# First tokens without the shift, and Fourier blocks with four products side by side

## The chip, the cores and the metric

The kernel runs on one core of one Trainium2 chip. Its time is the device time of one execution in microseconds (us). Before the change it took 2610.99 us (median of 3 runs, 2606.53 to 2611.72). The engines are TensorE (PE; PEld is its weight load), VectorE (DVE), ScalarE (ACT), GpSimd (POOL) and SyncE (SP); DMA queues of SP, ACT and POOL feed them.

## The reference

The kernel computes one block of a diffusion backbone, batch 1, 2048 latent tokens of 1024 channels, 256 context tokens. The part around the change:

```python
sh1, sc1, g1, sh2, sc2, g2 = ada_mod(c, w_ada, b_ada)   # silu(c) @ w_ada + b_ada, six pieces of 1024
hx = rms_norm(x, norm1_g) * (1 + sc1) + sh1
fx, qx, kx, vx = split_projection(hx @ w_in)            # four pieces of 512 columns
y_four = fourier_mix(fx)                                # 4 groups x 128 channels, fft2, real part
y_attn = neighbourhood_attention(rope(norm(qx)), rope(norm(kx)), vx, kc, vc, rpb)
mixed = merge(hx, y_four, y_attn, w_branch_gate, ...)   # gates = sigmoid(hx @ w_branch_gate)
x = x + g1 * mixed
x = x + g2 * sqrelu_mlp(rms_norm(x, norm2_g) * (1 + sc2) + sh2, w_mlp1, w_mlp2)
```

The context tokens give kc and vc in the same way, modulated by c_ctx.

## The kernel before, in words

**Tiling.** Channels lie on the 128 partitions in 8 chunks k, tokens in four groups of 512 ("quads"). A product of float32 values is three matmuls of high and low halves (`mm3`, the matmul itself is at L85): high by high, high by low, low by high. Halves are float16 scaled by powers of two, except for the first 512 tokens, whose products are made of fp32r halves that need no scale.

**Start.** `vec` gathers c, c_ctx, the gains and b_ada by five small transfers (L659 to L663, SP's queue); it is transposed (L680) and `sil` = silu(c) is made (L686). `ada_load` brings a 1 MB tile of w_ada, 8 input chunks by 256 columns; `ada_sum` multiplies the first chunks by sil on DVE and adds them (L278, L280, and L281 for the two partial sums); `ada_cols` lets PE take the other chunks as single-column products (L291), sum DVE's part over the partitions (L292), and DVE adds bias and gain (L294, L295). The result is column k of `AB`: columns 0 to 7 the shift, 8 to 15 the scale. Before, each of the 8 tiles holds 128 shift and 128 scale columns of one chunk, and from the third tile on DVE takes 6 input chunks and PE 2 (`PE_K = 6`).

**First 512 tokens.** `load_x` fetches 128 tokens, squares them (L201 on DVE, L203 on ACT), POOL takes the power (L175), and the tokens are scaled (L206, L208). `hx_k` makes chunk k of the modulated tokens: four transposes (L217), high half and full value on ACT with scale and shift (L220, L222), low half on DVE (L225). Then 12 products of that chunk go into four PSUM banks, `ps_first0` to `ps_first3` (128 Fourier channels each), with the first Fourier weights `w_first` in fp32r halves (L90, L93). So the first tokens run chunk by chunk, 96 products, as fast as the modulation columns arrive.

**Other tokens.** `norm_scale` (L250 to L263) finds the power of two for AB once all columns are there. `load_unit` does the same for 256 columns of weights: squares (L473), a power on POOL (L474), a sum over partitions on PE (L479), halves on ACT (L492) and DVE (L493). `build` makes the float16 halves of a quad: four transposes per chunk (L233), scale and shift on DVE or ACT (L237, L239), high half on ACT (L240), low half on DVE (L241). `unit_T` multiplies: one bank of 128 output channels at a time, 24 matmuls over all 8 chunks, and `put_T` (L501) takes the bank to memory. `first_tokens` rescales the first quad into float16 halves (L765, L767, L768).

**Order.** `run_pair(0)` takes the Fourier weights over quads 1, 2, 3, four banks after one another per quad, while the next quad is loaded and built. `run_pair(1)` to `run_pair(7)` take the other weights two units at a time over quads 0, 1, the context, 2, 3: gates, then q, v, k with gates among them. `side_work` (modulation for the context and the second sub-layer, 32 loads of MLP weights for scales, tile `w12m`, L324 to L328) is fed in between by `tick`. A scheduler estimates when each instruction could run and so sets the order of instructions on every engine; `tc.issue_after` pins one instruction behind another. PSUM has 4 banks for products ("mm"), 2 for transposes ("tp") and 1 for modulation sums, scales and other small results ("ad").

Of the kernel before, what the change touches and what calls it, by code (L numbers as in the profile page):

```python
# [66 lines left out]
def dit_block(ctx: ExitStack, tc: tile.TileContext, a, out, taps=None, upto=9):  # L67
# [126 lines left out]
    def load_x(src, r0, name, xh=None, sq_on_dve=False, scale_on_dve=False):  # L194
        if xh is None:
            xh = pb.tile([128, D], F32, tag="xh", name=f"xh_{name}", bufs=5)
        load(xh, src[r0:r0 + 128, :])
# [7 lines left out]
        if scale_on_dve:  # L205
            dve.tensor_scalar(out=xh, in0=xh, scalar1=rs, scalar2=None, op0=ALU.mult)  # L206
        else:
            act.activation(xh, xh, AF.Copy, scale=rs)  # L208
        return xh

    def hx_k(xhs, k, hx, ab, name, t_on_act=False):

        hH, hL = hx
        w = hH.shape[2]
        tp = tpp.tile([128, 512], F32, tag="tp", name=f"tp_{name}_{k}")[:, :w]
        for i, xh in enumerate(xhs):
            pe.transpose(tp[:, i * 128:(i + 1) * 128], xh[:, k * 128:(k + 1) * 128], ident)  # L217
        sc, bi = ab[:, 8 + k:9 + k], ab[:, k:k + 1]
        t = pb.tile([128, 512], F32, tag="ht", name=f"ht_{name}_{k}", bufs=2)[:, :w]
        h_ = act.activation(hH[:, k, :], tp, AF.Identity, bias=bi, scale=sc)  # L220
# [63 lines left out]
    def ada_cols(dst, j, c0, gain, name, acc, wt=None, nk=KT):  # L284

        ps = adp.tile([128, 512], F32, tag="ad", name=f"ad{name}")
        for i in range(2):
            bs = slice(i * 128, (i + 1) * 128)

            for k in range(nk, KT):  # L290
                pe.matmul(ps[:, i:i + 1], wt[:, k, bs], sil[:, k:k + 1], start=(k == nk), stop=False)  # L291
            pe.matmul(ps[:, i:i + 1], acc[:, bs], ones[:, 0:1], start=(nk == KT), stop=True)  # L292
# [2 lines left out]
        dve.scalar_tensor_tensor(out=dst[:, 8 + j:9 + j], in0=dst[:, 8 + j:9 + j], scalar=1.0, in1=gain,  # L295
                                 op0=ALU.add, op1=ALU.mult)
# [1685 lines left out]
```

## Time and profile before

| | before |
|---|---|
| median of 3 runs | 2610.99 us |
| the profiled execution | 2607.65 us, its span 2605.9 us |
| mean granted TensorE clock | 0.992 |
| PE busy / DVE / ACT / POOL | 96% / 70% / 45% / 17% |
| instructions | 42107 |
| last of the first-token products begins | 59.74 us |
| first product of quad 1 begins | 62.67 us |
| first gate product (`run_pair(1)`) begins | 158.9 us |

All times below are microseconds from the span's start. In rows of the timeline the columns are start, duration, engine, line, operation, out<-in, partitions, shape, type, count, and in brackets the idle time before it with what ended it; a row with a count above 1 is a run of equal instructions. A float32 product stands in the trace as two matmul records, a transpose or a 512-wide product as one: for a table of which PE takes two input chunks the program has per half two products of L291 and one of L292, and the trace shows x4 and x2. The change touches only the first 160 us of the span directly; the other 2446 us come after it.

### The profile page before, as it was taken

How to read it: one execution, taken by the hardware profiler on the slowest of the kernel's cores; microseconds unless marked ns; L12 is line 12 of the kernel's file. 1: busy time of each engine (PE TensorE's matmuls, PEld its weight loads, DVE VectorE, ACT ScalarE, POOL GpSimd, SP SyncE). 2: the span in 40 equal slices, each digit the busy share in tenths (PEclk: the TensorE clock that was granted, in tenths of full speed). 3: DMA queues.
4: the chain of work that ended last, by engine and by line, in shares of the span. 5: the costliest groups of instructions: out<-in, count | busy, mean ns of one | idle time of the engine just before them, and what ended most of it. 6: DMA issues, size and time to landing. Idle time of an engine off the chain costs nothing.

```text
span 2605.9 us, 42107 instructions
## 1 busy us (share of the span) xinstructions
PE 2512.3 (96%) x15839; PEld 1445.3 (55%) x15839; DVE 1814.5 (70%) x3738; ACT 1169.0 (45%) x2086; POOL 449.9 (17%) x560
## 2 busy tenths in 40 slices
PE   7899989899999899999999999999999999999999
PEld 5445656777655577786665444444444444444444
DVE  7656996686454788996775787979777534546367
ACT  5533236453144588883444655546360423224150
POOL 1210211002212447630000121211212000000000
PEclk9899999999999999999999999999999999999999
DMA  6456688773174586745667877776876433333334
GB/s 276 125 208 204 198 282 304 251 248 126 49 255 164 137 245 177 198 133 196 227 221 264 272 259 250 246 259 226 294 256 210 144 99 105 94 109 97 106 104 155
DMA packets 223125, 506.39 MB, mean 194 GB/s; under 512 B 31732, under 2 KB 85756, under 8 KB 207816
## 3 DMA queue, kind: packets, MB, share of 16 engines
q1 hardware_dynamic: 189960, 384.57, 45.7%
q0 software_dynamic: 26176, 87.90, 9.7%
q10 hardware_dynamic: 6784, 31.21, 3.6%
q8 instruction: 124, 2.03, 0.3%
q14 instruction: 81, 0.66, 0.1%
HBM read 366.22 MB, written 137.38 MB: 193 GB/s over the span
## 4 chain that ended last, share of the span: by engine, by line
PE 71%; DMA 11%; DVE 10%; ACT 4%; issue 3%; POOL 1%; SPq 1%; ACTq 0%; DVEq 0%; POOLq 0%
PE p L85 21%; PE pm L85 19%; PE ps_g L85 8%; PE po L85 5%; DMA w12m<-in_w_mlp 3%; PE ps_k L85 3%; PE pua L85 2%; PE tp L1413 2%; PE ps_f L85 2%; PE pv L1427 2%; PE pmf L1348 1%; DMA vt<-v 1%; PE sc L1391 1%; DVE wo L375 1%; PE ps_q L85 1%
## 5 line engine op out<-in xcount | busy, mean ns | idle before, releaser
L85 PE MATMUL pm<-hc,wb 128*128 128x512 f16 x2688 | 582.6, 379 | 5.5 <-DVE u L1697 3.5
L85 PE MATMUL p<-wb,a 128*128 128x512 f16 x2688 | 581.9, 379 | 2.0 <-DVE X L1697 1.5
L85 PEld LDWEIGHTS <-wb 128*128 128x128 f16 x2688 | 263.0, 98 | 323.5 <-issue 7.2
L85 PEld LDWEIGHTS <-a 128*128 128x128 f16 x2688 | 263.0, 98 | 319.7 <-issue 2.9
L85 PE MATMUL ps_g<-hx,w_g 128*128 128x512 f16 x1536 | 345.5, 380 | 1.0 <-DVE qn_q L563 1.0
L1697 DVE TENSOR_TENSOR X<-X,p 128x512 f32<-128x512 f32 x280 | 183.8, 682 | 171.0 <-PE p L85 151.7
L85 PEld LDWEIGHTS <-hx 128*128 128x128 f16 x2304 | 226.6, 99 | 36.1 <-issue 3.6
L85 PEld LDWEIGHTS <-w_g 128*128 128x128 f16 x1536 | 150.8, 100 | 167.6 <-issue 4.4
L85 PE MATMUL po<-wo,mH 128*128 128x512 f16 x512 | 152.4, 379 | 0.3 <-DVE ga L1471 0.3
L1697 DVE TENSOR_TENSOR u<-pm,u 128x512 f32<-128x512 f32 x128 | 87.3, 688 | 84.5 <-PE pm L85 82.4
L374 ACT ACTIVATE wo<-ws,msc 128x512 f16<-128x512 f32 x96 | 69.0, 718 | 163.7 <-DVE ws L415 128.2
L1400 DVE CUSTOM_DVE_ANT_0 s<-sc,bt,qsc 128x736 f32<-128x736 f32 (+5 forms) x128 | 111.1, 868 | 22.4 <-PE sc L1394 16.8
L1701 ACT ACTIVATE p<-pm 128x512 f32<-128x512 f32 x32 | 18.9, 589 | 239.7 <-PE pm L85 239.7
L1421 DVE SCALAR_TENSOR_TENSOR pL<-tp,pH 128x640 f16<-128x640 f32 (+1 forms) x128 | 112.3, 878 | 11.8 <-ACT pH L1416 11.0
L501 ACT ACTIVATE ot_g<-ps_g,usc_g 128x512 f32<-128x512 f32 x64 | 43.7, 683 | 164.5 <-PE ps_g L85 158.9
L1831 POOL DMA_DIRECT2D xr<-x1d x32 | 17.2, 539 | 569.4 <-DVE X L1697 563.1
L1404 ACT ACTIVATE s<-s,m 128x736 f32<-128x736 f32 (+5 forms) x128 | 104.6, 817 | 15.6 <-DVE m L1400 15.4
L1413 PE MATMUL tp<-ident,s 128*128 128x128 f32 x704 | 102.5, 279 | 3.8 <-ACT s L1404 3.7
L374 ACT ACTIVATE wo<-raw,msc 128x512 f16<-128x512 f32 x128 | 87.6, 709 | 38.1 <-issue 23.5
L375 DVE SCALAR_TENSOR_TENSOR wo<-raw,msc,wo 128x512 f16<-128x512 f32 x128 | 94.1, 744 | 8.4 <-ACT wo L374 8.4
L85 PE MATMUL po<-wo,mL 128*128 128x512 f16 x256 | 97.0, 379 | 0.0
L1416 ACT ACTIVATE pH<-tp 128x640 f16<-128x640 f32 (+1 forms) x128 | 95.8, 748 | 0.5 <-PE tp L1413 0.5
(568 smaller groups left out, 4369.4 us busy)
## 6 DMA issues: line engine op xcount, KB each, us to landing
wb<-w1d SPq DMA_DIRECT2D x224, 256.0 KB
wb<-w2d SPq DMA_DIRECT2D x224, 256.0 KB
w12m<-in_w_mlp SPq DMA_DIRECT2D x32, 1024.0 KB
raw<-in_w_mlp ACTq DMA_DIRECT2D x24, 1024.0 KB
w1d<-wo POOLq DMA_DIRECT2D x84, 256.0 KB, 3.8
w2d<-wo POOLq DMA_DIRECT2D x84, 256.0 KB, 4.0
gT<-ot_g SPq DMA_DIRECT2D x64, 256.0 KB
hc<-hcd SPq DMA_DIRECT2D x14, 1024.0 KB
```

The costliest lines, as they stand in the source:

```text
L85: last_mm[0] = pe.matmul(ps, l, r, start=(start and i == 0), stop=(stop and i == n - 1))
L374: act.activation(hi, src, AF.Copy, scale=scale)
L375: dve.scalar_tensor_tensor(out=lo, in0=src, scalar=scale, in1=hi, op0=ALU.mult, op1=ALU.subtract)
L501: last_out[0] = act.activation(o, ps, func, scale=scale)
L1348: pe.matmul(ps, l, r, start=(i == 0), stop=(i == len(prods) - 1))
L1400: tail["dve"] = dve.tensor_tensor_reduce(out=s[:, :n], in0=sc, in1=bias, op0=ALU.add, op1=ALU.min, scale=qsc[:, 4:5], scalar=3.0e38, accum ...
L1404: tail["act"] = act.activation(s[:, :n], s[:, :n], AF.Exp, bias=m1[:, 0:1], scale=-1.0, accum_out=m1[:, 1:2])
L1413: tail["pe"] = pe.transpose(tp[:, i * 128:(i + 1) * 128], s[:, o:o + 128], ident)
L1416: tail["act"] = act.activation(pH[:, :c], tp[:, :c], AF.Copy, scale=PTOP)
L1421: tail["dve"] = dve.scalar_tensor_tensor(out=pL[:, :c], in0=tp[:, :c], scalar=PTOP, in1=pH[:, :c], op0=ALU.mult, op1=ALU.subtract)
L1427: tail["pe"] = pe.matmul(pv, p_[:nk, i * 128:(i + 1) * 128], vv[:nk, h2 * 128 + o:h2 * 128 + o + 64], start=(j == 0 and i == 0), stop=(j = ...
L1697: last["dve"] = dve.tensor_tensor(out=o, in0=x, in1=y, op=op)
```

## The change

**Modulation tables.** They are packed so that tiles 0 to 3 hold 256 scale columns each (two chunks) and tiles 4 to 7 hold 256 shift columns each. `ada_cols` fills two scale columns or two shift columns per call. The share of input chunks that DVE sums becomes `PE_K = (0, 4, 6, 6, 4, 2, 0, 0)`, PE takes the rest: 0 means that PE does all 8.

**First tokens.** `hx_k` multiplies by the scale alone. The shift's part of the Fourier projection, the same for every token, is a column per 128 channels: 32 single-column products of the raw weights with the shift (`pshift`, L836), added as a bias when `put_T` evicts the four banks. For the later pairs `first_tokens` adds the shift (L871 to L874) into two rooms of their own, from where two SP transfers copy them into the room `hx0` (L878).

**Loads.** `vec` comes by ACT's queue. On SP's queue come the first tokens, table 0, half of the Fourier weights, table 1, the other half, tables 2 and 3, then the tokens of quad 1, tables 4 to 7, the tokens of quads 2 and 3. `load_x` is cut in `x_fetch` and `x_norm`.

**Fourier weights and quads 1 to 3.** `f_norm` and `f_split` (the float16 scale and halves of the Fourier weights) run among the first-token products. `quad(j)` runs the four banks side by side: for every chunk k twelve matmuls, three for each bank; `steps` builds the next quad's chunks beside (tp at L853, full value L857 or L859, high half L860, low half L861). All four token halves have rooms with tags of their own; quads 2 and 3 are normalised in quads 1 and 2.

The 512-wide products are the same in number. Single-column products for the first modulation columns go from 40 to 94 (16, 10, 6, 6, 10, 14, 16, 16 for tables 0 to 7), and `pshift` adds 32. The diff, cut:

```diff
-        h_ = act.activation(hH[:, k, :], tp, AF.Identity, bias=bi, scale=sc)
-        if t_on_act:
-            act.activation(t, tp, AF.Identity, bias=bi, scale=sc)
...
+        act.activation(hH[:, k, :], tp, AF.Copy, scale=sc)
+        h_ = act.activation(t, tp, AF.Copy, scale=sc)
...
-    sp.dma_start(vec[32:80, :], b_ada.rearrange("o (k p) -> (o k) p", p=128))
...
+    act.dma_start(vec[32:80, :], b_ada.rearrange("o (k p) -> (o k) p", p=128))
...
+    xhs = [x_fetch(x2, i * 128, f"00{i}") for i in range(4)]
     first_ada = {0: first_load(0)}
+    half_load(0)
+    first_ada[1] = first_load(1)
+    half_load(1)
+    for k in (2, 3):
+        first_ada[k] = first_load(k)
...
+    PE_K = (0, 4, 6, 6, 4, 2, 0, 0)
...
+    for k in range(KT):
+        if k % 2 == 0 and k + 2 < KT:
+            first_channels(k // 2 + 1)
+        if k + 1 < KT:
+            made.append(hx_k(xhs, k + 1, hx32, AB, "00"))
...
+        if k >= 4:
+            first_channels(k)
+        first_products(k)
+        if k == 2:
+            with after(*made[3]):
+                for u in range(2):
+                    f_norm(u)
+        if k == 4:
+            with after(*made[4]):
+                f_split(0)
+        if k == 5:
+            with after(*made[5]):
+                f_split(1)
...
+    for m in range(4):
+        for k in range(KT):
+            pe.matmul(ps[:, m:m + 1], raw_f[m // 2][:, k, (m % 2) * 128:(m % 2 + 1) * 128], shift[:, k:k + 1],
+                      start=(k == 0), stop=(k == KT - 1))
...
+    def quad(j, beside):
+        units = list(zip(f_w, f_usc))
+        ps = [mmp.tile([128, 512], F32, tag="mm", name=f"ps_f{m}_{j}") for m in range(4)]
+        for k in range(KT):
+            for m in range(4):
+                w, ms = units[m // 2][0], slice((m % 2) * 128, (m % 2 + 1) * 128)
+                mm3(ps[m], [(w[:, 0, k, ms], w[:, 1, k, ms], hx[j][:, 0, k], hx[j][:, 1, k])], k == 0, k == KT - 1)
+            beside(k)
+        for m in range(4):
+            put_T(ps[m], fT, m, j * 512, AF.Copy, f"f{m}_{j}", units[m // 2][1][:, 1:2], o=f_room(m, f"ot_f{m}_{j}"))
...
-        js = [0, 1, "c", 2, 3] if n else [1, 2, 3]
+        js = [0, 1, "c", 2, 3]
...
-    ada = [(o + k * 128, o + D + k * 128) for o in (0, 3 * D) for k in range(KT)]
+    ada = [(o + c,) for o in (0, 3 * D) for c in [*range(D, 2 * D, 256), *range(0, D, 256)]]
```

**Where instructions move.** On DVE, at the fourth table of scales. `aaccs3` and `aaccs4` are the sums of tables 3 and 4, `w_f0` and `w_f1` the low halves of the Fourier weights, the last row the columns of scale for chunks 6 and 7. Before (`aaccs4`, `aaccs5` the sums of the fifth and sixth table, `firstL` the low halves of the first tokens):

```order
L225 TENSOR_TENSOR firstL_211<-ht_00_2_319,firstH_210 128x512
L278 TENSOR_SCALAR aaccs4_344<-sparec_159,sil_120 128x256 x2
L280 SCALAR_TENSOR_TENSOR aaccs4_344<-sparec_159,sil_120,aaccs4_344 128x256 x2
L294 TENSOR_TENSOR AB_117<-ads3_352,vecT_121 128x2
L280 SCALAR_TENSOR_TENSOR aaccs4_344<-sparec_159,sil_120,aaccs4_344 128x256 x2
L295 SCALAR_TENSOR_TENSOR AB_117<-AB_117,vecT_121 128x1
L281 TENSOR_TENSOR aaccs4_344<-aaccs4_344 128x256
```

After (`hx_room2` and `hx_room3` are the high and low halves of the first tokens):

```order
L229 TENSOR_TENSOR hx_room3_160<-ht_00_5_445,hx_room2_159 128x512
L282 TENSOR_SCALAR aaccs4_449<-sparec_161,sil_120 128x256 x2
L284 SCALAR_TENSOR_TENSOR aaccs3_423<-hx_room1_158,sil_120,aaccs3_423 128x256 x2
L780 SCALAR_TENSOR_TENSOR w_f0_479<-ws_f0_163,usc_f0_382,w_f0_479 128x1024
L284 SCALAR_TENSOR_TENSOR aaccs4_449<-sparec_161,sil_120,aaccs4_449 128x256 x2
L780 SCALAR_TENSOR_TENSOR w_f0_479<-ws_f0_163,usc_f0_382,w_f0_479 128x1024
L284 SCALAR_TENSOR_TENSOR aaccs3_423<-hx_room1_158,sil_120,aaccs3_423 128x256
L780 SCALAR_TENSOR_TENSOR w_f1_525<-ws_f1_164,usc_f1_392,w_f1_525 128x1024 x2
L285 TENSOR_TENSOR aaccs4_449<-aaccs4_449 128x256
L285 TENSOR_TENSOR aaccs3_423<-aaccs3_423 128x256
L301 TENSOR_TENSOR AB_117<-ads3_431,vecT_121 128x2
```

The four low halves of the weights and the sum of table 4 now stand between the steps of table 3 and its end, ahead of the scale of chunks 6 and 7.

On PE, from the last first-token product to the first product of quad 1. Before (`pu_f` is the weights' norm, `tp_1_2` chunk 2 of quad 1):

```order
L85 MATMUL ps_first3_215<-firstL_211,w_first11_328 128x512
L85 MATMUL ps_first3_215<-firstH_210,w_first11_328 128x512
L479 MATMUL pu_f0_596<-usc_f0_592,ones_109 128x1
L233 MATMUL tp_1_2_643<-ident_104,x1_543 128x128 x4
L233 MATMUL tp_1_3_652<-ident_104,x1_543 128x128 x4
L479 MATMUL pu_f1_612<-usc_f1_608,ones_109 128x1
L85 LDWEIGHTS w_f0_603
L85 MATMUL ps_f01_0_709<-hx1_624,w_f0_603 128x512
```

After (`ads6`, `ads7` the last shift tables, `phsx` the sum of `norm_scale`):

```order
L853 MATMUL tp_1_0_700<-ident_104,hx_room0_157 128x128 x4
L853 MATMUL tp_1_1_709<-ident_104,hx_room0_157 128x128 x4
L295 MATMUL ads6_539<-sil_120,awts6_358 128x1 x16
L295 MATMUL ads7_569<-sil_120,awts7_360 128x1 x16
L262 MATMUL phsx_645<-hsmx_640,ones_109 128x1
L836 MATMUL pshift_654<-shift_638,ws_f0_163 128x1 x16
L836 MATMUL pshift_654<-shift_638,ws_f1_164 128x1 x16
L853 MATMUL tp_1_2_718<-ident_104,hx_room0_157 128x128 x4
L853 MATMUL tp_1_3_727<-ident_104,hx_room0_157 128x128 x4
L85 LDWEIGHTS w_f0_479
L85 MATMUL ps_f0_1_804<-hx_room1_158,w_f0_479 128x512
```

Two tables of shift, the norm's sum, the 32 products of `pshift` and 16 transposes now stand between the two; before, `phsx` and eight of the transposes were ahead of the last products.

On ACT, at the start of the build of quad 3. Before:

```order
L203 ACTIVATE xsq_31_1025,ss_31_1026<-xh_31_1023 128x1024
L208 ACTIVATE xh_31_1023<-xh_31_1023,rs_31_1030 128x1024
L473 ACTIVATE usq_g4_1183,usc_g4_1182<-ws_g4_951 128x2048
L501 ACTIVATE ot_f02_0_982<-ps_f02_0_957,usc_f0_592 128x512
L501 ACTIVATE ot_f02_1_1010<-ps_f02_1_985,usc_f0_592 128x512
L473 ACTIVATE usq_g5_1187,usc_g5_1186<-ws_g5_954 128x2048
L239 ACTIVATE ht_3_0_1059<-tp_3_0_1054,AB_117 128x512
```

After (`ot_f0_2` to `ot_f3_2` evict the four banks of quad 2, `t0` and `h0H` belong to `first_tokens`):

```order
L509 ACTIVATE ot_f0_2_1252<-ps_f0_2_1006,usc_f0_382 128x512
L871 ACTIVATE t0_6_1098<-hx_room3_160,AB_117,hsc_133 128x512
L871 ACTIVATE t0_7_1103<-hx_room3_160,AB_117,hsc_133 128x512
L509 ACTIVATE ot_f1_2_1255<-ps_f1_2_1007,usc_f0_382 128x512
L509 ACTIVATE ot_f2_2_1258<-ps_f2_2_1008,usc_f1_392 128x512
L509 ACTIVATE ot_f3_2_1261<-ps_f3_2_1009,usc_f1_392 128x512
L873 ACTIVATE h0H_844<-t0_6_1098 128x512
L873 ACTIVATE h0H_844<-t0_7_1103 128x512
L859 ACTIVATE ht_3_0_1141<-tp_3_0_1136,AB_117 128x512
```

The first chunk of quad 3 stands behind all four evictions of quad 2, which before came two at a time, and behind the first tokens' high halves.

More of the change, by code (lines that the diff above doesn't have):

```diff
@@ L444, in tick @@
         ticks[0] += pace[0]
-        with tc.issue_after(last_load[0].ins), tc.issue_after(last_out[0].ins) if side not in beside else nullcontext():
+        with tc.issue_after(last_load[0].ins), after(edge["dve"]), tc.issue_after(last_out[0].ins) if side not in beside else nullcontext():
             while ticks[0] >= 2:
@@ new lines, in dit_block @@
+    x_last = fetch_last()
+    ordered[0] = False
+    with after(*made[6]):
+        for i, t in enumerate(xh):
+            x_norm(t, f"01{i}", i >= 2, i >= 2)
+    shift = pb.tile([128, 12], F32, tag="hsb", name="shift")
+    dve.tensor_copy(shift[:, 0:8], AB[:, 0:8])
+    norm_scale(AB, 0, "x")
+    for u in f_usc:
+        dve.tensor_tensor(out=u[:, 1:2], in0=u[:, 5:6], in1=hsc[:, 1:2], op=ALU.mult)
+    ps = adp.tile([128, 512], F32, tag="ad", name="pshift")
+    for m in range(4):
+        for k in range(KT):
+            pe.matmul(ps[:, m:m + 1], raw_f[m // 2][:, k, (m % 2) * 128:(m % 2 + 1) * 128], shift[:, k:k + 1],
+                      start=(k == 0), stop=(k == KT - 1))
@@ new lines, in norm_quad, with first_pair, beside1, beside2 @@
+    def norm_quad(j, xh):
+        with after(edge["act"], edge["dve"]):
+            for i, t in enumerate(xh):
+                x_norm(t, f"0{j}{i}", i >= 2, i >= 2)
+    def first_pair():
+        new = [load_pair_unit(1, u) for u in range(2)]
+        tokens = first_tokens()
+        b1, b2, b3 = steps(1, hx_rooms[1], xh), steps(2, hx_rooms[0], x_late), steps(3, None, x_last)
+        for _ in range(4):
+            next(b1)
+        norm_quad(2, x_late)
+        for _ in b1:
+            pass
+        def beside1(k):
+            if k in (2, 3):
+                next(tokens)
+            if k >= 4:
+                next(b2)
+                next(b2)
+            if k == 7:
+                for o in new:
+                    next(o)
+        def beside2(k):
+            if k == 0:
+                norm_quad(3, x_last)
+            if k < 3:
+                next(tokens)
+                next(tokens)
+            if k == 3:
+                for _ in tokens:
+                    pass
+            if k >= 4:
+                next(b3)
+                next(b3)
+            if k == 5:
+                for o in new:
+                    next(o)
+        def beside3(k):
+            if k == 0:
+                for o in new:
+                    for _ in o:
+                        pass
+        quad(1, beside1)
+        quad(2, beside2)
+        quad(3, beside3)
@@ L801, in run_pair @@
                         turn(0)
[L802 to L808 removed]
+            for _ in range(j in (0, 1, 2)):
                 for o in new:
@@ L1079, in dit_block @@
         if n == 1:
-            with tc.issue_after(last_load[0].ins):
+            with tc.issue_after(last_load[0].ins), after(edge["act"], edge["dve"]):
                 load_gains()
```

228 lines of the change are left out of this document (142 added, 86 removed).

## The prediction

> **What bounds the kernel now.** I read the stages first. Columns: stretch, its length, busy time of PE, PEld, DVE, ACT and POOL, granted clock, DMA share, GB/s.
>
> ```profile
> 20.00:40.00 20.00, 19.34 (x91) 16.60 (x92) 19.51 (x52) 7.14 (x10) 0.00 (x0) 0.91 1.01 420
> 40.00:60.00 20.00, 19.96 (x117) 16.92 (x116) 15.79 (x47) 13.09 (x19) 5.35 (x6) 1.00 0.34 129
> 80.00:100.00 20.00, 10.38 (x44) 4.99 (x42) 13.75 (x20) 11.29 (x18) 4.70 (x5) 0.78 0.15 53
> 120.00:140.00 20.00, 13.34 (x72) 7.34 (x71) 17.36 (x41) 13.90 (x18) 12.99 (x8) 0.97 1.01 283
> ```
>
> PE is full from 20 to 60 (first tokens), has holes of 9.6 us in 80 to 100 and 6.7 us in 120 to 140 (quads 1 to 3). So two things can be won: PE work that could shrink before 60, and the holes. PE's waits up to 160 us name the holes:
>
> ```profile
> PE tp L233 <- ACT xh L208: 7.6, 2, 6.4
> PE ps_f L85 <- DVE hx L241: 4.3, 1, 4.3
> ```
>
> The norm of quad 2 costs 6.4 us in one piece, a late low half of quad 3 4.3 us. In the chain of waits the pair that follows is PE alone, and that gives the end of the touched part and two prices:
>
> ```profile
> 40.88 1.86 PE ps_first L85 x8
> 158.91 10.38 PE ps_g L85 x48
> 169.40 5.20 PE ps_g L85 x24
> ```
>
> An fp32r product costs 1.86/8 = 0.2325 us, a float16 one 5.20/24 = 0.2167. Since PE has no gap between these two rows (158.91 + 10.38 is 169.3) and keeps its order there under the change, what the first gate product moves by, the end moves by: I forecast that point.
>
> **Prices of small PE work.** PE's timeline:
>
> ```profile
> 11.26 1.02 PE L292 MATMUL ads<-ones,aaccs 128*128 128x1 f32 x4 [6.88 <-DVE aaccs L281]
> 20.41 2.08 PE L85 MATMUL ps_first<-firstH,w_first 128*128 128x512 f32 x4 [0.92 <-ACT firstH L220]
> 22.28 1.05 PE L217 MATMUL tp<-ident,xh 128*128 128x128 f32 x4
> 22.98 0.78 PE L85 MATMUL ps_first<-firstL,w_first 128*128 128x512 f32 x1
> 23.56 0.63 PE L85 MATMUL ps_first<-firstH,w_first 128*128 128x512 f32 x1
> 23.98 0.63 PE L85 MATMUL ps_first<-firstL,w_first 128*128 128x512 f32 x1
> 26.42 0.50 PE L292 MATMUL ads<-ones,aaccs 128*128 128x1 f32 x4
> 28.54 1.17 PE L85 MATMUL ps_first<-firstH,w_first 128*128 128x512 f32 x4
> 29.54 0.92 PE L217 MATMUL tp<-ident,xh 128*128 128x128 f32 x4
> 30.25 0.85 PE L291 MATMUL ads<-sil,spare 128*128 128x1 f32 x4
> 30.97 0.77 PE L85 MATMUL ps_first<-firstL,w_first 128*128 128x512 f32 x1
> 35.72 0.60 PE L217 MATMUL tp<-ident,xh 128*128 128x128 f32 x4
> 36.07 0.48 PE L85 MATMUL ps_first<-firstL,w_first 128*128 128x512 f32 x1
> 42.57 0.50 PE L291 MATMUL ads<-sil,sparer 128*128 128x1 f32 x4
> 43.83 1.18 PE L85 MATMUL ps_first<-firstH,w_first 128*128 128x512 f32 x4
> 59.74 0.40 PE L85 MATMUL ps_first<-firstH,w_first 128*128 128x512 f32 x1
> 62.67 1.04 PE L85 MATMUL ps_f<-hx,w_f 128*128 128x512 f16 x4 [1.36 <-ACT w_f L492]
> ```
>
> From 42.57 to 43.83 PE does one table's six single-column products (twelve records): 0.21 us each, nearly a full 512-wide product. A slow clock makes 512-wide ones 0.42 (23.56 to 23.98), single-column ones 0.36 (30.25 to 30.97, two of them) and transposes 0.175 instead of about 0.1 (22.28 to 22.98 and 35.72 to 36.07, four each). When it is slow, windows of 1 us tell:
>
> ```profile
> 29.00:30.00 1.00, 1.00 (x7) 0.83 (x6) 1.00 (x3) 1.00 (x3) 0.00 (x0) 0.84 1.01 426
> 30.00:31.00 1.00, 1.00 (x8) 1.00 (x6) 1.00 (x3) 1.00 (x3) 0.00 (x0) 0.50 1.05 442
> 33.00:34.00 1.00, 1.00 (x7) 0.82 (x6) 1.00 (x3) 0.00 (x0) 0.00 (x0) 0.95 1.01 426
> ```
>
> The clock falls to half at about 29.7, with PE busy, after 2.1 us mostly of single columns (26.42 to 28.54), 1 us of products and some transposes; it comes back near 33.1. So single columns and transposes don't hold it.
>
> **The change part by part.** *Start.* Table 0 comes behind 2 MB of tokens. At 420 GB/s they take 5.0 us; the five small transfers ahead of the first table are gone; I put it at 10.8. Now PE makes all 16 of its products (2 before), at the slow price 16 x 0.36 = 5.8: AB at about 17. With the transposes behind (8 x 0.175) and four products of table 1 (1.4), the first 512-wide product starts at about 20.2, against 20.41. Nothing is won.
>
> *First tokens.* From there 96 x 0.2325 = 22.3, 24 transposes 2.7, the 46 single columns of tables 1 to 5 that are left 46 x 0.21 = 9.7 (before 36 in all), two small norm products 0.4: 35.1. The slow clock at the start adds 2.8 (20.41 to 26.42: twelve products and four transposes in 6.0 us, 3.2 at full speed). DVE and ACT durations:
>
> ```profile
> 21.99 2.46 DVE L280 SCALAR_TENSOR_TENSOR aaccs<-spare,sil,aaccs 128x256 f32<-128x256 f32 x6
> 44.85 0.78 ACT L220 ACTIVATE firstH<-tp,AB 128x512 fp32r<-128x512 f32 x1 [3.04 <-DVE AB L295]
> 46.33 0.69 DVE L225 TENSOR_TENSOR firstL<-ht,firstH 128x512 fp32r<-128x512 f32 x1
> 46.94 0.42 DVE L281 TENSOR_TENSOR aaccs<-aaccs 128x256 f32<-128x256 f32 x1
> 64.59 1.28 DVE L493 SCALAR_TENSOR_TENSOR w_f<-ws_f,usc_f,w_f 128x1024 f16<-128x1024 f32 x1
> ```
>
> Now columns come in pairs of chunks. Chunks 2 and 4 wait for theirs (about 0.4 for the DVE steps, 0.75 for ACT, less what PE does meanwhile): 1.2. Chunk 6 waits longer: on DVE, four low halves of weights (4 x 1.28) and table 4's part stand ahead of table 3's end. From the low half of chunk 4 on (about 41.5) DVE has two low halves 1.3, ten steps (2.46/6 each) and two sums of both tables 4.9, the weights 5.1: about 11, so until 52 to 52.5. PE has run out of chunk 5 at about 47.8. Wait: 4.5. That idles the clock away, so table 3's and 4's 14 columns cost 0.15 more each (2.1) and the first eight products 0.2 more (1.6). Sum: 20.2 + 35.1 + 2.8 + 1.2 + 4.5 + 3.7 = 67.5. Before, the last of these ended at 60.1: 7.4 us lost.
>
> *Between.* Before, 2.6 us passed to the first product of quad 1 at 62.67. Now stand there, in PE's order: 8 transposes 0.9; 32 columns of shift, five quick and the others slow, 5 x 0.21 + 27 x 0.36 = 10.8; the chain of the norm on DVE, six steps of 0.15, 0.9; its product and `pshift`, 33 x 0.36 = 11.9; 8 transposes 1.4. Together 25.9, so quad 1 starts at 93.4: another 23.3 lost. The first four banks' eviction lies beside the transposes.
>
> *Quads 1 to 3.* 288 x 0.2167 = 62.4 of products, 80 transposes at 0.11 8.8, two norm products 0.4, a slow start of 1.4 (eight products). Four banks side by side need only chunk k of a new quad for 2.6 us of products, and the norms run a quad ahead, so the 6.4 and 4.3 us go. What is new is a wait at quad 3: its first chunk stands on ACT behind the last eviction and two high halves.
>
> ```profile
> L501 ACT ACTIVATE ot_f<-ps_f,usc_f 128x512 f32<-128x512 f32 x10 | 6.4, 680 | 9.3 <-PE ps_f L85 5.9 <-DMA fT<-ot_f 3.4
> L240 ACT ACTIVATE hx<-ht 128x512 f16<-128x512 f32 x16 | 9.4, 622 | 2.0 <-DVE ht L237 1.8
> L239 ACT ACTIVATE ht<-tp,AB 128x512 f32<-128x512 f32 x8 | 6.2, 772 | 16.0 <-PE tp L233 8.5 <-DVE hx L241 7.4
> ```
>
> 0.68 + 2 x 0.62 + 0.77 + 0.62 = 3.3, less 1 us of transposes that PE has: 2.3. Sum 75.3, where the stage took 158.9 - 62.7 = 96.2: 20.9 won. The first gate product: 93.4 + 75.3 = 168.7, 9.8 us later. Rescaling the first quad lies beside quads 1 and 2, and its copy is wanted 22 us (two times 10.38) after the gates of quad 1 could start, if at all; copying 2 MB at 420 GB/s is 5. Nothing else is on the path. Profiled 2607.65 + 9.8 = 2617.4; the median stands 3.3 above the profiled time, so 2610.99 + 9.8 = 2620.8.
>
> [...]
>
> **Rivals.** *The clock holds.* If single columns keep it up once it is up, tables 3 and 4 and the products behind lose their 3.7, the 59 slow columns between cost 0.15 less (8.9), the eight transposes and the product of the norm 0.7, and quad 1 starts warm (1.4): 14.7 in all, 9.8 - 14.7 = 4.9 faster, about 2606.1. Against it: the fall at 29.7. It turns to a gain once two thirds of the 14.7 come. *The wait on DVE doesn't occur,* because DVE keeps ahead: 4.5 + 3.7 = 8.2 less, 1.6 slower, 2612.6. Against it: DVE was full in 20 to 40 (19.51 of 20) and its order has the weights in front. *Dearer columns.* The first row above, 1.02 us for two, bounds a slow column at 0.5: 16 + 14 + 59 more at 0.14 each are 12, so 2633; or ACT and DVE are late for quads 2 and 3, up to the 10.7 us of the two old waits, 2631.5. *A later stage decides.* Around 360 to 480 PE idles and the loads of w12m are waited for:
>
> ```profile
> 360.00:400.00 40.00, 33.64 (x225) 22.58 (x224) 36.62 (x69) 9.42 (x28) 5.53 (x5) 0.91 0.86 282
> 400.00:440.00 40.00, 35.49 (x243) 23.70 (x241) 27.88 (x94) 26.95 (x42) 8.98 (x8) 1.00 0.90 304
> 440.00:480.00 40.00, 33.70 (x290) 28.36 (x289) 13.55 (x42) 24.97 (x42) 1.56 (x2) 0.96 0.89 300
> ```
>
> PE idles 17.2 us there. Orders of side work move in these pairs; if all of it went, the result would be 2603.6. DMA is 0.86 to 0.90 busy, so little can go.
>
> **How the numbers follow.** The forecast, 2615 to 2626, has 0.50; dearer columns or late quads 0.18; the DVE wait gone 0.13; the clock holding 0.12; the later stage 0.07. About 0.2% (5.2 us) can be told from no change. Slower: 0.50 + 0.18, less a little of the forecast's lower edge, 0.66. Same: the DVE rival and half of the clock one, 0.20. Faster 0.14. The range reaches from the clock rival to the dearer columns: 2605 to 2634.
>
> **What would show it.** In the changed profile: first 512-wide product at 20 to 21; a PE wait of 4 to 5 us for table 3's sum on DVE; the last first-token product at about 67; granted clock 0.5 over most of 70 to 93; quad 1 from about 93; a wait of about 2 us ahead of quad 3; the first gate product at about 169. If quad 1 starts before 80, the price of columns is wrong; if the gates start before 155, the sign is.

## The result, and the profile after

The changed kernel takes 2631.03 us (median of 4 runs, 2627.61 to 2640.71) beside 2608.76 us for the kernel before (4 runs, 2603.43 to 2611.72): a ratio of 1.0085, 95% interval 1.0067 to 1.0102. That is slower, by more than the 0.2% that can be told from no change. The page of the profiled execution:

```profile
span 2630.2 us, 42431 instructions
PE 2550.5 (97%) x16011; PEld 1483.3 (56%) x16011; DVE 1803.8 (69%) x3705; ACT 1170.2 (44%) x2096; POOL 449.5 (17%) x560
```

PE's share is higher than before, 97% against 96%, and the kernel is slower: PE counts as busy with small work at half clock (20.75 of the 22 us from 76 to 98, at 0.50). PE's timeline of the changed kernel, at the places that the forecast named:

```profile
12.16 6.99 PE L295 MATMUL ads<-sil,hx_room 128*128 128x1 f32 x32 [1.29 <-DVE sil L708]
22.32 2.05 PE L85 MATMUL ps_first<-hx_room,w_first 128*128 128x512 f32 x4
53.84 0.38 PE L297 MATMUL ads<-ones,aaccs 128*128 128x1 f32 x2 [2.25 <-DVE aaccs L285]
68.08 1.40 PE L85 MATMUL ps_first<-hx_room,w_first 128*128 128x512 f32 x5
70.19 3.63 PE L295 MATMUL ads<-sil,awts 128*128 128x1 f32 x32
74.07 6.99 PE L295 MATMUL ads<-sil,awts 128*128 128x1 f32 x32 [0.25 <-DVE AB L301]
82.06 0.56 PE L262 MATMUL phsx<-hsmx,ones 128*128 128x1 f32 x2 [0.99 <-DVE hsmx L260]
82.87 13.81 PE L836 MATMUL pshift<-shift,ws_f 128*128 128x1 f32 x64 [0.25 <-DVE hsc L264]
96.54 1.95 PE L853 MATMUL tp<-ident,hx_room 128*128 128x128 f32 x8
98.28 5.49 PE L85 MATMUL ps_f<-hx_room,w_f 128*128 128x512 f16 x18
151.25 0.33 PE L853 MATMUL tp<-ident,xh 128*128 128x128 f32 x1 [3.81 <-ACT ht L859]
152.50 4.39 PE L85 MATMUL ps_f<-hx,w_f 128*128 128x512 f16 x12
176.88 10.52 PE L85 MATMUL ps_g<-hx,w_g 128*128 128x512 f16 x48
```

Two rows stand one behind the other and are the same amount of work: table 6 takes 3.63 us for 16 columns, table 7 takes 6.99. Between them the clock fell, as windows of 1 us tell. Windows of the changed kernel (columns as in the prediction: stretch, length, busy PE, PEld, DVE, ACT, POOL, granted clock, DMA share, GB/s):

```profile
72.00:73.00 1.00, 1.00 (x11) 1.00 (x11) 0.00 (x0) 0.00 (x0) 0.00 (x0) 1.00 0.21 82
73.00:74.00 1.00, 0.82 (x8) 0.73 (x7) 0.14 (x1) 0.00 (x0) 0.00 (x0) 0.94 0.00 0
74.00:75.00 1.00, 0.93 (x5) 0.93 (x5) 0.02 (x1) 0.00 (x0) 0.00 (x0) 0.50 0.00 0
76.00:98.00 22.00, 20.75 (x97) 20.61 (x98) 3.87 (x16) 3.01 (x5) 0.00 (x0) 0.50 0.15 50
```

From 74 to 98 PE is busy for 94% of the time and its clock is half (0.50), with the weight loads (PEld) as full as PE (22.54 us and 22.68). Stage by stage, from the starts of the groups in one profiled execution of each kernel (the last product of the first tokens ends at 68.08 + 1.40 = 69.5):

| stretch, us | before | forecast | after | missed by |
|---|---|---|---|---|
| start to the first 512-wide product | 20.4 | 20.2 | 22.3 | 2.1 |
| first tokens | 39.7 | 47.3 | 47.2 | -0.1 |
| between, to quad 1 | 2.6 | 25.9 | 28.8 | 2.9 |
| quads 1 to 3, to the first gate product | 96.2 | 75.3 | 78.6 | 3.3 |
| first gate product to the end of the span | 2447.0 | 2447.0 | 2453.3 | 6.3 |
| span | 2605.9 | 2615.7 | 2630.2 | 14.5 |

**The last line** is where the forecast had nothing. From the first gate product to the last product of the key projection (`ps_k`) both kernels take the same, 574.8 and 575.6 us. From there to the last gate product the kernel before takes 111.0 us (733.6 to 844.6) and the changed one 118.1 (752.5 to 870.6). SP's queue there, before and then after (start, duration, issue):

```profile
749.86 0.60 SPq L1105 DMA_DIRECT2D chan<-in_chan  x1
750.50 0.43 SPq L897 DMA_DIRECT2D X<-fT  x1
```

```profile
769.25 0.61 SPq L1274 DMA_DIRECT2D chan<-in_chan  x1
774.09 0.33 SPq L1066 DMA_DIRECT2D X<-fT  x1
```

The load of the first Fourier block, X, is issued 0.6 us after the one ahead of it in the kernel before, and 4.8 us after it in the changed one. SP's queue names what that issue waits for there, the landing of a copy of the halves of k:

```profile
SPq L1066 <- DMA kHL<-sH_k: 4.2, 1, 4.2
```

Tiles moved in memory, and X's room now follows rooms that are still being copied out. In that pair PE waits for products made of X (PE's waits, before and then after; total, times, longest):

```profile
PE pc L856 <- DVE eL L843: 2.0, 1, 2.0
```

```profile
PE pc L1025 <- DVE eL L1012: 3.4, 1, 3.4
PE pc L1025 <- DVE fsc L250: 0.8, 1, 0.8
```

and its clock falls around those waits, to 0.79 and 0.87, where before it stays at 1.00. The window of before with its 2.0 us, and then two of after:

```profile
803.60:813.60 10.00, 8.17 (x47) 4.83 (x47) 6.47 (x18) 7.16 (x14) 2.05 (x2) 1.00 0.52 165
```

```profile
822.50:832.50 10.00, 6.61 (x34) 4.46 (x34) 3.00 (x10) 5.98 (x10) 1.08 (x1) 0.79 0.68 249
832.50:842.50 10.00, 10.00 (x51) 5.48 (x50) 7.15 (x29) 5.45 (x8) 2.01 (x2) 0.87 0.40 136
```

### The profile page after: what moved, and what is told of

The parts are those of the page before. It is cut to its first block, busy times and chain, and to the rows that moved or that the text cites. A ratio compares the mean times of both kernels' runs of the same rounds, so it can differ in the third digit from the quotient of the medians.

```text
span 2630.2 us, 42431 instructions
## 1 busy us (share of the span) xinstructions
PE 2550.5 (97%) x16011; PEld 1483.3 (56%) x16011; DVE 1803.8 (69%) x3705; ACT 1170.2 (44%) x2096; POOL 449.5 (17%) x560
## 4 chain that ended last, share of the span: by engine, by line
PE 74%; DVE 10%; DMA 8%; ACT 4%; issue 3%; SPq 1%; POOL 0%; ACTq 0%; DVEq 0%; POOLq 0%
PE p L85 21%; PE pm L85 19%; PE ps_g L85 8%; PE po L85 6%; PE ps_k L85 2%; PE ps_f L85 2%; PE pua L85 2%; PE tp L1582 2%; DMA w12m<-in_w_mlp 2%; PE pv L1596 1%; PE pmf L1517 1%; DMA raw<-in_w_mlp 1%; PE sc L1560 1%; PE psq L85 1%; PE ps_q L85 1%
## 5 line engine op out<-in xcount | busy, mean ns | idle before, releaser
L85 PE MATMUL ps_g<-hx_room,w_g 128*128 128x512 f16 x768 | 178.4, 389 | 1.0 <-DVE qn_q L571 1.0
L85 PE MATMUL ps_g<-hx,w_g 128*128 128x512 f16 x768 | 172.2, 379 | 0.3 <-DVE qn_k L571 0.3
L85 PEld LDWEIGHTS <-hx_room 128*128 128x128 f16 x1152 | 112.5, 98 | 21.4 <-issue 4.4
L85 PEld LDWEIGHTS <-hx 128*128 128x128 f16 x1152 | 112.8, 99 | 15.7 <-issue 0.9
L1590 DVE SCALAR_TENSOR_TENSOR pL<-tp,pH 128x640 f16<-128x640 f32 (+1 forms) x128 | 112.5, 879 | 11.8 <-ACT pH L1585 10.9
```

The source lines that it names most:

```text
L85: last_mm[0] = pe.matmul(ps, l, r, start=(start and i == 0), stop=(stop and i == n - 1))
L1590: tail["dve"] = dve.scalar_tensor_tensor(out=pL[:, :c], in0=tp[:, :c], scalar=PTOP, in1=pH[:, :c], op0=ALU.mult, op1=ALU.subtract)
```

## Experiments

All start from the changed kernel unless said otherwise. Gate is the start of the first gate product, 176.9 in the changed kernel and 158.8 before, both by the timeline (the chain of waits has 158.9 before). Landmarks are of one profiled execution each, and runs without an interval are single executions.

**One: without `pshift`.** The 32 products and the bias are left out; the first tokens' Fourier columns then lack the shift's part.

```diff
-    for m in range(4):
-        for k in range(KT):
-            pe.matmul(ps[:, m:m + 1], raw_f[m // 2][:, k, (m % 2) * 128:(m % 2 + 1) * 128], shift[:, k:k + 1],
-                      start=(k == 0), stop=(k == KT - 1))
...
-        put_T(first[m], fT, m, 0, AF.Identity, f"first{m}", bias=shift[:, 8 + m:9 + m], o=f_room(m, f"ot_first{m}"))
+        put_T(first[m], fT, m, 0, AF.Copy, f"first{m}", o=f_room(m, f"ot_first{m}"))
```

> Leaves out the 32 single-column products of pshift and the bias made of them, so the first 512 tokens lack the shift's part in their Fourier columns. In the changed kernel these products take 13.8 us of the 29 between the last first-token product (ends 69.5) and quad 1 (98.3). If they set the start of quad 1 alone, quad 1 starts at 84 to 85 and the first gate product at 162 to 164 (176.9 with them). If something beside them holds quad 1 as well (the build of its chunks, the evictions that free the banks), it moves by less than 8.

Measured: quad 1 at 87.1, gate 164.7, 2608.93 us. Quad 1 comes 11.1 us earlier for 13.8 us of products: 2.0 are taken by a new wait for the build of chunk 2 on ACT, which `pshift` had hidden, and the first tokens of this execution ended 0.9 later. The gate moves by 12.2, the span by 23.1 (2607.1): 4.7 of the other 10.9 us are in the last gate pair (113.4), 5.1 between the gates and the keys (570.5). Neither lies in the stretch where `pshift` stood, and one execution doesn't tell how much of it would come again.

**Two: tables 6 and 7 summed on DVE.**

```diff
-    PE_K = (0, 4, 6, 6, 4, 2, 0, 0)
+    PE_K = (0, 4, 6, 6, 4, 2, 8, 8)
```

> Tables 6 and 7 (the last shift columns) are summed by DVE whole, PE takes 2 products of each in place of 16. In the changed kernel PE spends 70.2 to 81.1 on them while DVE is idle (0.2 us busy of 4 in 68 to 76). If it is PE's single columns that count, DVE does its 2 x 3.4 us between 62 and 71, quad 1 starts at 86 to 89 and the first gate product at 165 to 168. If DVE's sums only take their place as a wait, quad 1 stays within 3 us of 98.3.

Measured: quad 1 at 88.4, gate 166.0, as expected, 2623.6 us. Twenty-eight columns go here (two sums over partitions of each table stay). From the end of the first tokens to quad 1 it takes 20.1 us instead of 28.8, and in the first run, where 32 other columns went, 16.8: 0.31 and 0.38 us less per column, each net of a wait that took their place (1.2 for DVE here, 2.0 for ACT there). So most of the gap is single columns, whatever they compute.

**Three: wide products between the columns,** to see whether they bring the clock up. One 512-wide product, whose result nobody reads, after every second column of `pshift`:

```diff
+            if k % 2:
+                w = w_first[k // 4, m // 2]
+                pe.matmul(fill, w[:, 0, k % 4, 0:128], hx32[0][:, k, :], start=True, stop=True)
```

> Work is only added: after every second product of pshift PE makes one 512-wide product whose result nobody reads (16 of them, 3.7 us at full clock). If single columns are dear because the clock falls under them, the wide ones bring it back within about 4 us: the stretch from the first product of pshift to quad 1 gets shorter or stays (15.4 us before; 11 to 15 now), the granted clock is 1.00 in the last part of it, and quad 1's first 18 products take about 3.9 instead of 5.3. If the price does not come from the clock, the stretch gets 3.7 (full clock) to 6.8 us (half) longer.

Inconclusive: the scheduler put the sixteen products at 58, 69 and 75 us, none of them between the columns (2626.51 us). Pinned in place, each behind its column and ahead of the next one:

```diff
+            with after(prev) if prev else nullcontext():
+                prev = pe.matmul(ps[:, m:m + 1], raw_f[m // 2][:, k, (m % 2) * 128:(m % 2 + 1) * 128], shift[:, k:k + 1],
+                                 start=(k == 0), stop=(k == KT - 1))
+            if k % 2:
+                w = w_first[k // 4, m // 2]
+                with after(prev):
+                    prev = pe.matmul(fill, w[:, 0, k % 4, 0:128], hx32[0][:, k, :], start=True, stop=True)
```

> The fillers again, now pinned: two single-column products of pshift, one 512-wide product nobody reads, sixteen times (in the run before the scheduler had put the fillers elsewhere). 3.7 us of work are added at full clock, 6.8 at half. If the clock is what makes the columns dear, and if a third of wide products is enough to bring it back (not known: in the kernel before about 60% were wide), the stretch of pshift lasts 12 to 14 us instead of 13.8 and quad 1's first 18 products 3.9 to 4.3 instead of 5.5. If the clock stays at half, or is not the cause, the stretch lasts 17 to 21.

PE's timeline of that kernel and a window of it:

```profile
82.38 1.02 PE L839 MATMUL pshift<-shift,ws_f 128*128 128x1 f32 x4 [0.25 <-DVE hsc L264]
83.26 0.77 PE L844 MATMUL fill<-hx_room,w_first 128*128 128x512 f32 x1
83.83 0.85 PE L839 MATMUL pshift<-shift,ws_f 128*128 128x1 f32 x4
84.54 0.77 PE L844 MATMUL fill<-hx_room,w_first 128*128 128x512 f32 x1
```

```profile
80.00:104.00 24.00, 22.76 (x90) 20.99 (x91) 4.25 (x15) 3.36 (x5) 0.00 (x0) 0.50 0.14 48
```

One group of two columns and a wide product takes 1.28 us (83.26 to 84.54). A wide product takes 0.42 us at a clock of 0.50 in the kernel before, from start to start:

```profile
31.54 0.63 PE L85 MATMUL ps_first<-firstH,w_first 128*128 128x512 f32 x1
31.96 0.63 PE L85 MATMUL ps_first<-firstL,w_first 128*128 128x512 f32 x1
```

```profile
31.00:32.00 1.00, 1.00 (x4) 0.81 (x5) 1.00 (x3) 1.00 (x2) 0.00 (x0) 0.50 0.95 401
```

Here 0.57 pass from its start to that of the next column, so wide products filled 33 to 45% of the time. The clock, at half when `pshift` began, stayed at 0.50 for the whole stretch, which took 20.7 us instead of 13.7 from its first column to the transposes behind it; quad 1 came at 107.6, the time was 2639.07 us. That share of wide work didn't bring the clock back here; what share would, these runs don't show.

**Four: the four banks one after another** in `quad`. With the loops each bank's eviction and the steps that run beside the products move too: two steps stand behind each bank now. The diff is cut to the loops.

```diff
-        for k in range(KT):
-            for m in range(4):
+        for m in range(4):
+            for k in range(KT):
```

> The changed kernel with the four banks of a quad one after another again (all eight chunks for one bank, then the next). If side by side is what took the holes out of quads 1 to 3, a bank now needs all chunks of its quad before its end, the quad's build shows as PE waits of 5 us and more at each quad's start, and from quad 1's first product to the first gate product it takes 84 to 95 us instead of 78.6. If the order of the banks is worth nothing, it stays at 77 to 80.

Measured: gate 190.8, 2647.37 us. From quad 1 to the gates it takes 92.9 us instead of 78.6, in the range expected, but not by the waits expected, 5 us and more at each quad's start. PE waits there are three:

```profile
PE tp L853 <- ACT ht L859: 7.3, 1, 7.3
PE adc L297 <- DVE usc_g L251: 5.0, 1, 5.0
PE adc L297 <- DVE ABc L301: 3.7, 1, 3.7
```

One quad, the third, waits for its build, 7.3 us instead of 3.8. The other 8.7 us are two tables of the context's modulation (`adc`) that now stand ahead of the first gate product on PE and wait for DVE; in the changed kernel they come at 187 us, behind it, without a wait. So this edit costs 14.3 us, but the banks' order as such shows in 3.5 us of them, and 8.7 come of a shift of side work; the 2.1 left stand in no wait.

**Five: `pshift` and tables 6 and 7 on DVE,** so that PE has a few sums over partitions in place of 64 columns.

```diff
-    PE_K = (0, 4, 6, 6, 4, 2, 0, 0)
+    PE_K = (0, 4, 6, 6, 4, 2, 8, 8)
...
+            if k < 2:
+                dve.tensor_scalar(out=o, in0=raw_f[u][:, k, :], scalar1=sc, scalar2=None, op0=ALU.mult)
+            else:
+                dve.scalar_tensor_tensor(out=o, in0=raw_f[u][:, k, :], scalar=sc, in1=o, op0=ALU.mult, op1=ALU.add)
```

> Tables 6 and 7 on DVE as in the run e2_tables_dve (quad 1 at 88.4), and pshift's weighted sums over the eight chunks on DVE too (sixteen steps and two sums, about 7.3 us, and four single-column products on PE in place of 32). PE's 13.8 us become a wait of 7 to 9 us for DVE: quad 1 starts at 80 to 84, the first gate product comes at 157 to 162. If DVE is what limits this stretch, quad 1 stays at 88 or later.

Measured: quad 1 at 87.0, gate 165.4, 2615.82 us, later than expected. The stretch between the first tokens and quad 1 does what was expected, 14.0 us instead of 28.8; the first tokens end late, at 73.0 instead of 69.5, with a wait of 3.8 for table 3 and slow products behind it: 19 of them took 7.45 us from 59.42, where 19 x 0.2325 are 4.4. PE's waits between 60 and 90:

```profile
PE pshift L844 <- DVE aaccf L842: 3.8, 1, 3.8
PE phsx L262 <- DVE hsmx L260: 2.7, 1, 2.7
```

The slow columns are gone, and 6.5 us of waits for DVE stand in their place.

**Six: the weights' halves later,** behind table 3's end on DVE.

```diff
-        if k == 4:
-            with after(*made[4]):
+        if k == 6:
+            with after(*made[7]):
                 f_split(0)
-        if k == 5:
-            with after(*made[5]):
                 f_split(1)
```

> The float16 halves of the Fourier weights are made after chunk 7's low half instead of after chunks 4 and 5; nothing else. The prediction's account of the wait for table 3 (DVE's queue) has it vanish: no PE wait for its sum (2.2 us in the changed kernel, with the clock falling behind it), the last first-token product at 64 to 67 instead of 69.1, quad 1 2 to 5 us earlier. If the wait comes from the table's landing or from the sums themselves, it stays.

Measured: the wait for table 3 is gone, the last first-token product begins at 62.9 instead of 69.1, quad 1 at 94.1, gate 173.0, 2620.55 us. So the queue on DVE that the prediction described is real, and 5.7 us of the first tokens (41.1 instead of 46.8 from first to last product) come of a wait of 2.2 and the slow clock behind it (0.57 from 56 to 64). Three other profiles have PE's and DVE's order of the changed kernel up to there (experiments one, four and the changed kernel of nine): 46.6 to 48.2 us from first to last product, with waits of 2.2 to 3.8, so the gain is 5.5 to 7.1.

**Seven: the old start with the new quads.** The first tokens are as before the change (scale and shift in one tile, shift added in `hx_k`, `vec` on SP's queue, no `pshift`); rooms, fetches and the side-by-side quads are those of the change.

```diff
-    PE_K = (0, 4, 6, 6, 4, 2, 0, 0)
+    PE_K = 6
...
-    ada = [(o + c,) for o in (0, 3 * D) for c in [*range(D, 2 * D, 256), *range(0, D, 256)]]
+    ada = [(o + k * 128, o + D + k * 128) for o in (0, 3 * D) for k in range(KT)]
```

> Half of the change: the modulation tables, the order of loads and the first tokens as in the kernel before (128 shift and 128 scale columns in a table, shift in the tokens, no pshift), quads 1 to 3 with four banks side by side as in the changed one. If the two halves add up, the first tokens end near 60, quad 1 starts at 63 to 68 and the first gate product comes at 141 to 148: 11 to 18 us faster than before, ratio 0.993 to 0.996. If the side-by-side quads lived on the 29 us that DVE and ACT had ahead of quad 1, they now wait for their builds and the ratio is 0.998 to 1.001.

Measured: 2596.85 us (4 runs), beside 2608.91 for the kernel before: ratio 0.9957, interval 0.9940 to 0.9974. It beats both kernels. First tokens end as before, quad 1 starts at 66.3, the gates at 142.5, 16.3 us ahead of the kernel before. From quad 1 to the gates it takes 76.2 us, where the forecast's sum has 75.3 and the kernel before took 96.1; the start of quad 1 is 3.6 later. Its waits in the quads are those for the build, 3.4 and 2.7 us:

```profile
PE tp L827 <- ACT ht L833: 3.4, 2, 3.0
PE tp L827 <- DVE ht L831: 2.7, 1, 2.7
```

So the change is two changes of opposite sign: at the first gate product the quads win 16.3 us, and the start and first tokens lose 34.4 (142.5 to 176.9), against 20.9 and 30.7 in the forecast.

**Eight: scale first, all repairs at once:** five, six, table 0 on DVE and `vec` on SP's queue.

```diff
-    act.dma_start(vec[32:80, :], b_ada.rearrange("o (k p) -> (o k) p", p=128))
+    sp.dma_start(vec[32:80, :], b_ada.rearrange("o (k p) -> (o k) p", p=128))
...
+    PE_K = (8, 4, 6, 6, 4, 2, 8, 8)
```

> The changed kernel with everything the earlier runs priced put right together: table 0 and the last two tables summed by DVE, pshift's sums on DVE, the float16 halves after chunk 7, vec on SP's queue ahead of the tokens. If the losses are those terms and add up, the first 512-wide product comes at 17 to 19 (22.3), the last first-token product at 56 to 60, quad 1 about 15 later at 71 to 75, the first gate product at 149 to 154, and the whole takes about 2596 to 2603. If taking the scales of two chunks at a time is itself the loss, the first tokens still end after 62 and the gates come after 157.

A miss: 2619.43 us. The first product comes at 20.6 instead of 22.3 (17 to 19 expected), but quad 1 comes at 85.5 and the gates at 163.6. Most of it is missed in the first tokens: the last of their products begins at 68.5, where 56 to 60 was expected and experiment six had 62.9. PE hardly waits there (0.2 us idle between 52 and 68); its clock fell (0.66 from 52 to 56, 0.50 from 56 to 60 and from 64 to 68, 0.93 between). The same sixteen products in experiment six and then here:

```profile
54.37 3.96 PE L85 MATMUL ps_first<-hx_room,w_first 128*128 128x512 f32 x16
```

```profile
55.57 6.03 PE L85 MATMUL ps_first<-hx_room,w_first 128*128 128x512 f32 x16
```

So what was expected if pairs of scales are the loss came true (an end after 62, gates after 157), but not for that reason, since experiment six takes the scales in pairs too. Whether the repairs or the single execution brought the clock down, one run doesn't tell. From the end of the first tokens to quad 1 it takes 16.4 us, near the 15 expected. There DVE is the bound, and PE with next to nothing to do (busy for 2.48 of 8 us) is at half clock:

```profile
76.00:84.00 8.00, 2.48 (x11) 2.42 (x12) 7.59 (x28) 1.10 (x2) 0.00 (x0) 0.50 0.23 59
```

The repairs don't add up to the forecast of this run. Between the first tokens and quad 1 they move the same vector products from PE at half clock to a DVE that is full.

**Nine: X's room.** Two unused tiles ahead of it lay X elsewhere; nothing else changes, and PE's order up to the gates is that of the kernel without the edit.

```diff
+        for i in range(2):
+            ff.tile([128, 4, 512], F32, tag="fold", name=f"foldx{i}", bufs=2)
         x_rooms = (x_room.rearrange("p k n -> p (k n)"), ff.tile([128, S], F32, tag="X", name="X"))
```

On the mixed kernel of experiment seven, twice on different chips (the second run is the same program again), and on the changed kernel:

> The run e8_old_start_new_quads with one thing moved: in the pool of the early Fourier blocks the two rooms of fold come ahead of the room of X. In the changed kernel, as in all the runs so far, X's transfer waits for writes of k to have landed (3 to 5 us between the transfer of chan and that of X, 0.04 before), because X's room took over rooms that these still read; now it should not. If that wait is why the last pair of gates is longer (117 us from the last product of k to the last gate in e8, 111 before), it goes to 111 to 114, and the whole is 3 to 6 us faster than e8: ratio to before 0.9935 to 0.995. If the last pair is longer for another reason, it stays at 115 to 118 and the ratio at 0.9957.

> The mixed kernel (old start and first tokens, new side-by-side quads: 2596.85 us) with the same single edit of X's room and nothing else. Theory: its first gate stays near 142.5, its last pair of gates falls from 117 to 113 or 114, and the time to 2592 to 2595. Rival (the gap doesn't matter): last pair 117, time 2596 to 2598.

> The changed kernel with one edit, far behind the touched stage: two unused tiles are taken ahead of X's room, so that the room of the first Fourier block X is laid elsewhere in memory and takes over no room that is still being copied out. In the changed kernel the transfer of X begins 4.8 us after that of the channel matrix in front of it in SP's queue (769.25 and 774.09), before the change 0.6 us. Theory (X is late, so the channel products and their halves come in a bunch, PE waits 3.4 us for one of them and its clock falls): the gap goes below 2 us, the last pair of gates (first to last, ps_k's last product to ps_g's last) takes 112 to 115 us instead of 118, and the time is 3 to 6 us below the changed kernel's, 2625 to 2628. Rival (the gap doesn't matter; the last pair is longer for another reason, such as the order of the side work): the gap goes, the last pair stays at 117 to 119, the time stays at 2630 to 2632. Landmarks up to 752 should be those of the changed kernel in either case.

Measured: mixed 2598.37 us (4 runs, ratio 0.9949, interval 0.9929 to 0.9969) and 2597.76 (6 runs, 0.9962, 0.9944 to 0.9981); changed 2631.61 (4 runs, 1.0084, 1.0064 to 1.0105). The gap on SP's queue falls to 1.9, 0.8 and 1.9 us; for the changed kernel, with what X's issue waits for now:

```profile
778.10 0.61 SPq L1276 DMA_DIRECT2D chan<-in_chan  x1
779.98 0.33 SPq L1068 DMA_DIRECT2D X<-fT  x1
```

```profile
SPq L1068 <- DMA fw<-in_w_fourier_rev: 1.2, 1, 1.2
```

The last gate pair takes 113.9, 110.5 and 111.4 us. With the gap (2.9 to 5.2 us, ten profiles of this study) it takes 112.3 to 118.1, on average 115.7; without it 110.5 to 113.9, the kernel before among them, on average 111.7. The ranges touch, but with the room moved the pair is shorter in each of the three (by 3.1, 6.5 and 6.7 us against the kernel without the edit), so X's room, and with it the late load, makes that pair longer, by some 4 us on average over the profiles. Yet none of the three ratios falls by more than 0.1%. Their intervals reach about 5 us to either side, so a gain of 4 us isn't refuted by them either; it doesn't show. Where it may go can be seen only in single profiles. In the changed kernel with the moved room the clock fell earlier in the single columns:

```profile
69.00:70.00 1.00, 1.00 (x5) 0.76 (x5) 0.07 (x1) 0.00 (x0) 0.00 (x0) 0.79 0.00 0
70.00:71.00 1.00, 1.00 (x6) 0.80 (x5) 0.00 (x0) 0.00 (x0) 0.00 (x0) 0.50 0.00 0
```

so both tables were slow (table 6 took 6.83 us where it had taken 3.63), and quad 1 began at 103.3 instead of 98.3; 0.8 of these 5.0 us were there before, at the last first-token product (69.9 instead of 69.1). In the second mixed run attention's scores took 306.0 us from first to last start instead of 297.4. The two mixed runs, one program, differ by 4.1 us in the start of quad 1 (69.7 and 65.6). These are differences between executions, as large as the gain that was looked for. That X's room costs the pair time is shown; that it costs the kernel time is not.

## Why the prediction was right, and where its size was off

The forecast was 2620.8, in a range of 2605 to 2634, and the kernel came out at 2631.03: slower, as forecast, but by 22 us where the sum had 9.8. That is above the forecast's own 2615 to 2626, in the part that had 0.18 for dearer columns or late quads, and both came in part. Point by point, by the steps on record.

- *First product at 20 to 21*: 22.3. The price that failed is the start of table 0's columns, put at 10.8 by the tokens' transfer. The columns wait for `sil` instead, and `vec` comes late on ACT's queue, beside the tokens (on SP's queue, in experiment eight, PE has it at 3.95). The chain of waits of the changed kernel:

```profile
4.37 5.94 DMA vec<-in_b_ada
10.51 0.38 PE pvec L702
12.16 6.99 PE ads L295 x32
```

  Sixteen columns then took 6.99 us, not 5.8. That is 0.44 each, as much as at 0.50 further on, but the granted clock reads 1.00 there (12.16 to 19.15). It reads 1.00 before the change too, from 20.00 to 26.40, where the prediction speaks of a slow clock: the products there took 0.42 us each (23.56 to 23.98), and no run shows why.

- *First tokens, 47.3*: 47.2, by two errors that cancel. The wait for table 3 was 2.2 us and not 4.5; experiment six puts it and the slow clock behind it at 5.7 instead of 8.2. The other terms were about as much too short. The two hang together: PE ran out of work at 51.6 and not at 47.8, because the first product was 2.1 later and the clock, at 0.83 between 30 and 50, took by estimate some 2 us more, and DVE's sum was ready at 53.8. In experiment one and in the changed kernel of experiment nine the same order waits 3.8; in experiment one PE ran out of work at 48.5, 26.7 us behind its first product, where it is 29.3 here. So the mechanism is the one forecast, the rival without this wait is refuted, and that the stage came out to 0.1 us is luck. The sum also has four columns of table 1 twice (0.8 us), in the start and among the 46.

- *Clock 0.5 over most of 70 to 93*: 0.50 from 74 to 98. The rival "the clock holds" is refuted: it would have taken 14.7 us off, and even wide products in between (experiment three) didn't raise it from half (0.50 from 80 to 104). The size of the step was off: a slow column was priced at 0.36, from a row of two columns with a wide product behind them. In a row of their own they take 13.81/32 = 0.43 us. For the 33 behind the norm that is 2.4 us, the main part of the 2.9 missed. The 32 columns of tables 6 and 7 took 10.6 us where 10.8 were counted, but by luck: sixteen quick ones and sixteen at 0.44, not five and 27 at 0.36. Experiment three, with two columns and then a wide product, gives 0.36 again (83.83 to 84.54, halved), so each price holds for its arrangement. The rival "dearer columns" took 0.5 as its bound and comes nearest in time (2633), which is luck too: columns make less than a third of what was missed.

  The same order of work on PE saw the clock fall at 74 in one execution and at 70 in another. PE busy for 94% of 24 us, mostly in single columns, didn't hold the clock up: it was 0.50 all that time.

- *A wait of 2 us ahead of quad 3*: 3.8, and the clock fell behind it (1.00 from 146 to 152, 0.57 from 152 to 156), so the twelve products at 152.50 took 4.39 us where 2.6 were counted. The wait's 1.5 too much and these 1.8 are about the 3.3 of that stage: the step counted the wait and not the slow clock behind it, which it had counted for table 3. The eight products of the slow start, 1.4 in that sum, are shown by no run as such; the first 18 products of quad 1 took 5.49 us, 1.6 more than 18 x 0.2167. The old waits of 6.4 and 4.3 us are gone, as the step said, and the mixed kernel's 76.2 us agree with the sum's 75.3. Of the step's two reasons, norms a quad ahead and banks side by side, the first does more: with the banks one after another (experiment four) the wait for the norm of quad 2 doesn't come back, and the wait for a build is 3.5 us longer. No run leaves out the early norms alone.

- *"What the first gate product moves by, the end moves by"*: this step is off in the profile by 6.3 us, and it had no term for what changed. The first gate product comes 18.0 us later and the span ends 24.3 later. PE's order there is kept, as the prediction argued, but not the place of tiles in memory, and so not the time at which a load may start. Experiment nine shows the room's part in the pair, about 4 us; that all of the 6.3 is due to it isn't shown, since the time didn't fall with the room moved. One pair of profiles doesn't fix the size either: in the ten profiles with the gap this stretch takes 2442.4 to 2455.5 us, on average 2450.5, and the one of the kernel before, 2447.0, lies within. The medians are 22.3 us apart, which leaves an estimate of some 4 us behind the gate.

- *The later stage*, a gain of up to 17 us around 360 to 480: nothing came; the stretch from gates to keys took 575.6 us against 574.8.

## What to carry to other kernels

Price single-column products that stand together by the dozen by such a bunch, not by a row among wide products: here each of the 32 of `pshift` cost 0.43 us at a clock of 0.50, against 0.21 at 1.00 (42.57 to 43.83 before), and the products behind them started slow too (18 in 5.49 us, at 0.50 from 98 to 100 and 0.70 from 100 to 102). When a change bundles two edits, run each alone: here the half with the side-by-side quads was 0.4% faster than the kernel before, and the whole was 0.85% slower. After a change of tile sizes or tags, look far behind it for loads that now wait for another room.

## What the runs showed of the hardware

The granted clock went to 0.50 with PE and its weight loads busy for 94% of 24 us, and stayed there with 33 to 45% of the time in wide products (experiment three, 80 to 104); in the changed kernel sixteen columns took 3.63 us (clock 1.00), and the next sixteen 6.99 (0.50). The sixteen at 12.16 took 6.99 us as well, at a granted clock of 1.00. When the clock falls within such a stretch varied by 4 us between two executions with the same order of work on PE (74 and 70), and that moved quad 1 by 4 of 5 us. Among the first tokens it was 0.83 between 30 and 50 us in the changed kernel. With the same order of work on PE, the wait behind that stretch was 2.2 us there and in experiment four, and 3.8 in experiment one and in the changed kernel of experiment nine.
